# Row norms by a power on GpSimd, and a new order of loads, squares and weight splits, in a two-layer decoder trunk

## The chip, the cores and the metric

The kernel runs on one core of a Trainium2 chip. The metric is the device time of one execution in microseconds (us), as the median of several executions; lower is better. Five engines work side by side, each through its own queue in order: PE (TensorE, matrix products and transposes), ACT (ScalarE), DVE (VectorE), POOL (GpSimd) and SP (SyncE, which here only issues transfers).

## The reference

512 tokens of width 1024 pass two layers. All data are float32.

```python
def rms_norm(x, g):
    y = xf * lax.rsqrt(jnp.mean(xf * xf, axis=-1, keepdims=True) + RMS_EPS)
    return y * g
...
    for layer in range(DEPTH):                  # DEPTH = 2
        if layer == N_CONV_LAYERS:              # layer 1
            k_sh, v_sh = shared_kv(h, positions, kv_norm, w_kv)
        hn = rms_norm(h, mix_norm_pre[layer])
        if layer < N_CONV_LAYERS:
            y = short_conv_mixer(hn, conv_w_in[layer], conv_w[layer], conv_w_out[layer])
        else:
            y = dilated_attention_mixer(hn, positions, k_sh, v_sh, w_q[j], w_o[j])
        h = h + rms_norm(y, mix_norm_post[layer])
        f = swiglu(rms_norm(h, ffn_norm_pre[layer]), ffn_w_gate_up[layer], ffn_w_down[layer])
        h = h + rms_norm(f, ffn_norm_post[layer])
    return h
```

So each token row is normed before and after each mixer and each feed-forward part, and a norm needs one number for each row: one over the root of the mean square. The norm ahead of the shared keys and values is of the same `h` as the one ahead of layer 1, so eight such numbers are needed for each row.

## The kernel before

The 512 tokens stand as four tiles of 128 rows, 0 to 3; the 1024 columns of a tile are worked in two halves, a and b. Every weight is split when it has arrived: `raw` (the load, 1 MB for two matrices' columns), `wh` (a rounded copy that ACT makes, L90) and `wl` (the rest, a subtraction on DVE, L91). Activations are split in the same way into `xh` and `xl`. A product is then three matmuls, `xh` with `wh`, `xh` with `wl` and `xl` with `wh`.

A norm of tile 3, say, goes through four engines. ACT squares the two halves and sums each row (`square`, L190; `ssn` for the sums of a norm behind a block, `ssx` for those of a norm ahead of one). `rsqrt_mean` (L193 to L207) turns the two sums of a row into the reciprocal root: seven small instructions on one number in each of 128 rows, which form the sum `a`, a first guess from the integer bits, and two polishing steps. They run on POOL, but on DVE for tiles 0 and 1 at the start of the program and for tile 3 at its end. DVE then scales the row: `yg` times the result plus `h` (L268) for a norm behind a block, `hn` (L225, or L228 with a gain) for one ahead of a block. PE transposes `hn` (`tr`, L236), and `split` makes `xh` and `xl` of it.

Where one block ends and the next begins (a stage border), the class `Next` runs these steps tile by tile while PE still works on the old block's last tiles. A tile goes through two norms in series there: `add` (the norm of the block's output y, and the residual sum), then `norm` and `x` for the next block. The next block's first products are made in halves: `feature_mms` takes four weight splits ("makers") in turn and makes each one's product for tiles 0 and 1 alone (`between` says where the transposes of tiles 2 and 3 stand, which is behind the second and the fourth of these), then the products for tiles 2 and 3. There are three such borders: convolution to feed-forward (at 197 to 212 us of the profile), feed-forward to attention (563 to 590) and attention to feed-forward (1113 to 1166); the program's start and its end are of the same kind.

Work is put into the queues by a scheduler that goes by its own estimates of times. `behind(marks)` holds a piece of work back, in the order of issue alone, until the instructions in `marks` have been issued. Before, the first pair of makers stood behind tile 0's square and scaling, the second pair behind nothing:

```python
            if i % 2 == 0:
                with behind(marks[i // 2]):
                    pairs += [m() for m in makers[i:i + 2]]
```

At the start, SP issues all loads in the order tile 0 of `h`, the gain row `g0`, `ident` (for the transposes), tile 1, the first weight, and so on. PE runs eight matmuls on zeros (`warm`), spreads `g0` over 128 rows (`g0a`, `g0b`), and runs one more on zeros.

Of the kernel before, what the change touches and what calls it, by code (L numbers as in the profile page):

```python
# [15 lines left out]
P = 128  # L16
T = 512
# [21 lines left out]
def trunk(  # L39
# [42 lines left out]
    cols = keep.tile([P, 64], F32, name="cols")  # L82
    taps, gq, gkv = cols[:, 0:24], cols[:, 24:32], cols[:, 32:40]

    def bank(tag, name):
        return psum.tile([P, T], F32, tag=tag, name=name)

# [52 lines left out]
    @contextmanager  # L140
    def behind(marks):

        with ExitStack() as stack:
            for m in marks:
                stack.enter_context(tc.issue_after(m))
            yield

    def feature_mms(makers, between=None, attn=False, marks=((), ())):

        half = NT // 2
        if between is None:
            pairs = [m() for m in makers]
            for i in range(0, len(pairs), 2):
                feature_mm(pairs[i:i + 2], 0, NT, attn)
            return [ps for ps, _ in pairs]
        pairs = []
        for i in range(len(makers)):
            if i % 2 == 0:  # L160
                with behind(marks[i // 2]):
                    pairs += [m() for m in makers[i:i + 2]]
            feature_mm([pairs[i]], 0, half, attn)
            for f in between[i]:
                f()
# [18 lines left out]

    HALF = [slice(0, 512), slice(512, 1024)]

    def square(pool, y, ssq):
# [5 lines left out]
    def rsqrt_mean(pool, ssq, tag, eng=nc.gpsimd):  # L193
# [12 lines left out]
        eng.tensor_scalar(t, y, a, y, ALU.mult, ALU.mult)  # L206
        eng.tensor_scalar(y, t, -RS ** 10 * 64.0 / 3.0, y, ALU.add, ALU.mult)  # L207
        return y

    def row_gain(pool, g):  # L210
# [2 lines left out]
            nc.sync.dma_start(t, g.partition_broadcast(P))  # L213
        return t

    def norm_x(pool, tt, gain, eng=nc.gpsimd):

        ssq = pool.tile([P, 2], F32, tag="ssx", name="ssx")
        for i, c in enumerate(HALF):
            square(pool, h[:, tt, c], ssq[:, i:i + 1])  # L220
        hn = pool.tile([P, D], F32, tag="hg", name="hn", bufs=3)
        r = rsqrt_mean(pool, ssq, "x", eng)
        for i, c in enumerate(HALF):
            if gain is None:
                nc.vector.tensor_scalar(hn[:, c], h[:, tt, c], r, None, ALU.mult)  # L225
            else:
                g = gain[i] if isinstance(gain, list) else gain[:, c]
                nc.vector.scalar_tensor_tensor(hn[:, c], h[:, tt, c], r, g, ALU.mult, ALU.mult)  # L228
        return hn

    def to_x(tt, hn, attn=False):
# [14 lines left out]
    class Next:  # L246
# [3 lines left out]
        def __init__(self, pool, ys, gpost, gpre, n=0):  # L250
            self.pool, self.ys, self.n = pool, ys, n
            self.gpost, self.gpre = (g if g is None else row_gain(pool, g) for g in (gpost, gpre))
            self.hn, self.ssq, self.yg, self.marks = {}, {}, {}, {}

        def add(self, tt, n, eng=nc.gpsimd):

            y, c = self.ys[tt][n], HALF[n]
            if n == 0:
                self.ssq[tt] = self.pool.tile([P, 2], F32, tag="ssn", name="ssn")
                self.yg[tt] = self.pool.tile([P, D], F32, tag="hg", name="yg", bufs=3)  # L260
            yg = self.yg[tt]
            marks = [square(self.pool, y, self.ssq[tt][:, n:n + 1]),
                     nc.vector.tensor_tensor(yg[:, c], y, self.gpost[:, c], ALU.mult).ins]
            if n == 1:
                self.marks[tt] = marks
                r = rsqrt_mean(self.pool, self.ssq[tt], "n", eng)
                for c in HALF:
                    nc.vector.scalar_tensor_tensor(  # L268
                        h[:, tt, c], yg[:, c], r, h[:, tt, c], ALU.mult, ALU.add)

        def norm(self, tt):
            self.hn[tt] = norm_x(self.pool, tt, self.gpre)

        def x(self, tt):
            to_x(tt, self.hn.pop(tt), self.gpre is None)
# [101 lines left out]
    with ExitStack() as phase:  # L377
# [23 lines left out]
        nc.sync.dma_start(rows[32:40, :], kv_norm.rearrange("(c p) -> c p", p=P))  # L401

        zeros = up.tile([P, T], BF16, name="zeros")
        nc.vector.memset(zeros, 0.0)
        idle = bank("at", "idle")

# [14 lines left out]
        with tc.issue_after(mark):  # L421
            for tt in range(2):
                marks0 = to_x(tt, hn0[tt])
# [6 lines left out]
        for c in range(KT // 2):  # L430
# [346 lines left out]
    with ExitStack() as phase:  # L777
# [23 lines left out]

        class Last(Next):
            def after_half(self, tt, n):
                self.add(tt, n, nc.vector if tt == NT - 1 else nc.gpsimd)
                if n == 1:
                    for c in HALF:
# [48 lines left out]
```

## Time and profile before

| what | value |
|---|---|
| median of 3 executions | 1523.56 us (1521.35 to 1524.08) |
| profiled execution, its own time | 1523.93 us |
| span of the profiled execution, first to last instruction | 1522.1 us |
| PE busy | 1495.3 us, 98% of the span |
| DVE, ACT, POOL busy | 49%, 40%, 7% of the span |
| mean granted TensorE clock | 0.994 |

The span is 1.8 us shorter than the time; that much lies around the first and the last instruction. PE is the engine that is nearly always busy, so what another engine does counts where PE stands still for it, and where PE's clock is lower for having stood still. The granted clock is given as a share of 2.4 GHz; 0.5 is 1.2 GHz.

### The profile page before, as it was taken

The page shows a single profiled execution, that of the slowest core. Times are in us where ns is not written, and L with a number is a line of the kernel's source. Part 1 is how long each engine was busy: PE and PEld are TensorE (multiplying, and loading weights), DVE is VectorE, ACT ScalarE, POOL GpSimd, SP SyncE. Part 2 cuts the span into 40 slices and gives each one's busy share as a digit, 9 for nine tenths or more (in the row PEclk, how much of TensorE's full clock was granted, in tenths as well). Part 3 has the DMA queues.
Part 4 walks back from the last instruction along what each step waited for, and adds up shares of the span by engine and source line. Part 5 has one row for each costly group of instructions (what it writes and reads, how often), then busy time and mean ns, then how long its engine had stood idle before and what let it go on. Part 6 is the DMA issues. An engine that isn't in the chain of part 4 may idle for free.

```text
span 1522.1 us, 20115 instructions
## 1 busy us (share of the span) xinstructions
PE 1495.3 (98%) x8158; PEld 1262.2 (83%) x8158; DVE 745.4 (49%) x1328; ACT 616.4 (40%) x1137; POOL 108.1 (7%) x247
## 2 busy tenths in 40 slices
PE   8999999999999998999999999999998999999997
PEld 7888888888888887898788889889877888888886
DVE  5644453323234366776667566765554322223333
ACT  4323342212123244664666557557553221212321
POOL 2000320000000051000001001000023000000001
PEclk9999999999999999999999999999999999999999
DMA  6333123133323312322112222212040323332311
GB/s 210 111 112 110 56 94 127 62 106 111 124 87 107 111 38 74 111 85 80 61 58 85 84 73 69 84 56 84 30 138 24 124 76 111 111 109 99 111 56 56
DMA packets 109330, 137.43 MB, mean 90 GB/s; under 512 B 3469, under 2 KB 97973, under 8 KB 109238
## 3 DMA queue, kind: packets, MB, share of 16 engines
q1 hardware_dynamic: 107958, 135.89, 27.1%
q8 instruction: 64, 1.05, 0.3%
q0 software_dynamic: 1280, 0.26, 0.2%
q14 instruction: 28, 0.23, 0.0%
HBM read 133.92 MB, written 2.23 MB: 89 GB/s over the span
## 4 chain that ended last, share of the span: by engine, by line
PE 68%; issue 24%; POOL 5%; DVE 1%; ACT 1%; DMA 0%; SPq 0%; DVEq 0%; ACTq 0%; POOLq 0%
PE mmf L137 27%; PE atf L137 14%; PE vps L649 10%; PE s L580 3%; PE o L708 2%; PE tr L679 2%; POOL t L203 1%; POOL a L197 1%; POOL yi L205 1%; POOL q L204 1%; POOL t L206 1%; PE y L182 1%; PE y L180 1%; PE y L178 1%; DVE hn L228 0%
## 5 line engine op out<-in xcount | busy, mean ns | idle before, releaser
L91 DVE TENSOR_TENSOR wl<-raw,wh 128x1024 fp32r<-128x1024 f32 x244 | 292.7, 1222 | 70.7 <-ACT wh L90 70.4
L90 ACT CAST wh<-raw 128x1024 fp32r<-128x1024 f32 x244 | 246.7, 1047 | 100.7 <-PE atf L137 43.1
L137 PE MATMUL mmf<-xh,wh 128*128 128x512 f32 (+1 forms) x848 | 277.4, 380 | 0.2 <-ACT xh L90 0.2
L137 PE MATMUL mmf<-xl,wh 128*128 128x512 f32 (+1 forms) x848 | 271.2, 374 | 0.0
L137 PE MATMUL mmf<-xh,wl 128*128 128x512 f32 (+1 forms) x848 | 271.0, 374 | 0.0
L137 PE MATMUL atf<-xh,wh 128*128 128x512 f32 (+1 forms) x560 | 181.8, 368 | 0.0
L137 PE MATMUL atf<-xl,wh 128*128 128x512 f32 (+1 forms) x560 | 180.1, 365 | 0.0
L137 PEld LDWEIGHTS mmf<-xh,wh 128*128 128x128 f32 x848 | 154.7, 191 | 30.6 <-issue 2.1
L137 PE MATMUL atf<-xh,wl 128*128 128x512 f32 (+1 forms) x560 | 180.0, 365 | 0.0
L362 DVE TENSOR_TENSOR act<-atf,s 128x512 f32<-128x512 f32 x44 | 30.5, 692 | 304.1 <-ACT s L361 304.1
L137 PEld LDWEIGHTS mmf<-xl,wh 128*128 128x128 f32 x848 | 153.2, 188 | 28.8 <-issue 0.9
L137 PEld LDWEIGHTS mmf<-xh,wl 128*128 128x128 f32 x848 | 153.5, 189 | 27.7
L361 ACT ACTIVATE s<-mmf 128x512 f32<-128x512 f32 x44 | 26.3, 598 | 336.3 <-PE mmf L137 336.3
L110 DVE TENSOR_TENSOR raw<-raw,cols 128x512 f32<-128x512 f32 x144 | 90.2, 686 | 78.6 <-DMA raw<-in_w_kv 56.2
L137 PEld LDWEIGHTS atf<-xh,wh 128*128 128x128 f32 x560 | 100.6, 191 | 17.0
L137 PEld LDWEIGHTS atf<-xl,wh 128*128 128x128 f32 x560 | 99.6, 189 | 16.8
L137 PEld LDWEIGHTS atf<-xh,wl 128*128 128x128 f32 x560 | 99.5, 189 | 16.8
L527 ACT COPY sw<-mmf 32x512 f32<-32x512 f32 x92 | 53.3, 579 | 79.4 <-PE mmf L137 72.2
L649 PE MATMUL vps<-wh,xh 128*128 128x256 f32 x384 | 81.1, 289 | 0.0
L649 PE MATMUL vps<-wh,xl 128*128 128x256 f32 x384 | 79.3, 286 | 0.0
L649 PE MATMUL vps<-wl,xh 128*128 128x256 f32 x384 | 79.1, 285 | 0.0
L91 DVE TENSOR_TENSOR al<-act,ah 128x512 fp32r<-128x512 f32 x44 | 30.2, 691 | 93.9 <-ACT ah L90 93.9
(192 smaller groups left out, 2058.6 us busy)
## 6 DMA issues: line engine op xcount, KB each, us to landing
raw<-in_ffn_w_gate_up SPq DMA_DIRECT2D x44, 1024.0 KB, 7.5
raw<-in_w_kv SPq DMA_DIRECT2D x24, 1024.0 KB, 5.2
raw<-in_ffn_w_down SPq DMA_DIRECT2D x22, 1024.0 KB, 4.9
raw<-in_conv_w_in SPq DMA_DIRECT2D x12, 1024.0 KB, 5.2
raw<-in_w_q SPq DMA_DIRECT2D x12, 1024.0 KB, 5.2
raw<-in_conv_w_out SPq DMA_DIRECT2D x4, 1024.0 KB, 4.8
raw<-in_w_o SPq DMA_DIRECT2D x4, 1024.0 KB, 5.0
h<-in_x SPq DMA_DIRECT2D x4, 512.0 KB, 8.9
```

Of the source, the lines that this page charges most:

```text
L90: return [nc.scalar.copy(hi, src).ins, nc.vector.tensor_tensor(lo, src, hi.bitcast(F32), ALU.subtract).ins]
L91: nc.vector.tensor_tensor(lo, src, hi.bitcast(F32), ALU.subtract).ins]
L110: nc.vector.tensor_tensor(src[:, ks], src[:, ks], g.broadcast_to([P, a // 2, b]), ALU.mult)
L137: nc.tensor.matmul(ps, (wh, wl, wh)[p][:, k, :], x[p == 2][:, k], start=i == 0, stop=i == len(todo) - 1)
L178: nc.tensor.matmul(o, ah, wh[i], start=first, stop=False)
L361: nc.scalar.activation(s, ps[2 * j], AF.Silu)
L362: nc.vector.tensor_tensor(act[2 * c + j], ps[2 * j + 1], s, ALU.mult)
L527: nc.scalar.copy(w[s:s + 32], y[s + 32:s + 64])
L580: nc.tensor.matmul(ps[h2][:, b - b2, e * P:(e + 1) * P], q[pr][rw, b * P:(b + 1) * P], k[pr][rw, kb * P:(kb + 1) * P], start=True, stop=True)
L649: nc.tensor.matmul(ps[m][:, n, :], (zh, zh, zl)[p][:, k, 2 * m + n], (wh, wl, wh)[p], start=k == 0 and p == 0, stop=k == KT - 1 and p == 2)
L679: nc.tensor.transpose(tr[:, b - b2, e:e + P], p[:, e - lo:e - lo + P], ident)
L708: m = nc.tensor.matmul(out, v, rhs, start=first, stop=part == 0 and e == 1, skip_group_check=True).ins
```

## The change

It has four parts. (1) `rsqrt_mean` becomes two POOL instructions: the sum `a`, and `a` to the power of -0.5, the exponent being a column of constants (`mhalf`). The rows that DVE took before (tiles 0 and 1 at the start, tile 3 at the end) move to POOL as well. (2) At the start, `g0` and `ident` are issued by ACT; tile 1 of `h` is issued directly behind tile 0; the first weight arrives in two loads of 128 columns each; there are 4 + 2 warming matmuls for 8 + 1; the second half's square of tiles 0 and 1 is made on DVE. (3) Each of the four makers gets a mark of its own: at a border, the first and the second wait as before for tile 0's square and scaling (the first pair did), the third for tile 3's residual sum, the fourth for tile 3's `hn`. (4) The very last output transfer is issued by ACT instead of SP.

```diff
-    def feature_mms(makers, between=None, attn=False, marks=((), ())):
+    def feature_mms(makers, between=None, attn=False, marks=((),) * 4):
...
-                with behind(marks[i // 2]):
-                    pairs += [m() for m in makers[i:i + 2]]
+                for m, mark in zip(makers[i:i + 2], marks[i:i + 2]):
+                    with behind(mark):
+                        pairs.append(m())
...
+        if junk is not None:
+            return nc.vector.tensor_tensor_reduce(
+                junk, y, y, 1.0 / 1024.0, 0.0, ALU.mult, ALU.add, ssq).ins
...
-        eng.tensor_scalar(a, ssq[:, 0:1], EPS, ssq[:, 1:2], ALU.add, ALU.add)
-        yi = pool.tile([P, 1], I32, tag=tag + "y", name="yi")
-        eng.tensor_scalar(yi, a.bitcast(I32), -0.5, -553033664.0, ALU.mult, ALU.add)
-        y = yi.bitcast(F32)
-        t = pool.tile([P, 1], F32, tag=tag + "t", name="t")
-        q = pool.tile([P, 1], F32, tag=tag + "q", name="q")
-        eng.tensor_scalar(t, y, a, y, ALU.mult, ALU.mult)
-        eng.tensor_scalar(q, t, -RS ** 2 * 10.0 / 3.0, t, ALU.add, ALU.mult)
-        eng.tensor_scalar(y, q, RS ** 4 * 5.0, y, ALU.add, ALU.mult)
-        eng.tensor_scalar(t, y, a, y, ALU.mult, ALU.mult)
-        eng.tensor_scalar(y, t, -RS ** 10 * 64.0 / 3.0, y, ALU.add, ALU.mult)
+        nc.gpsimd.tensor_scalar(a, ssq[:, 0:1], EPS, ssq[:, 1:2], ALU.add, ALU.add)
+        y = pool.tile([P, 1], F32, tag=tag + "y", name="y")
+        nc.gpsimd.tensor_tensor(y, a, mhalf, ALU.pow)
         return y
...
-                    "marks": [self.marks[0], ()]}
+                    "marks": [self.marks[0]] * 2 + [[self.added[NT - 1]], self.normed[NT - 1]]}
...
+        nc.scalar.dma_start(g0, mix_norm_pre[0:1, :])
+        nc.scalar.dma_start(ident, consts[:, 0:P])
         for tt in range(NT):
             nc.sync.dma_start(h[:, tt, :], x[0, tt * P:(tt + 1) * P, :])
-            if tt == 0:
-                nc.sync.dma_start(g0, mix_norm_pre[0:1, :])
-                nc.sync.dma_start(ident, consts[:, 0:P])
             if tt == 1:
-                first.append(load_cols(w, D))
+                raw = wp.tile([P, KT, 256], F32, tag="raw", name="raw")
+                for j in range(2):
+                    cs = slice(j * P, (j + 1) * P)
+                    latest[:] = [nc.sync.dma_start(
+                        raw[:, :, cs], w[:, D:][:, cs].rearrange("(k p) n -> p k n", p=P)).ins]
+                first.append(raw)
...
-        with tc.issue_after(warm(8)):
+        with tc.issue_after(warm(4)):
...
-            mark = warm(1)
-
-        hn0 = [norm_x(npool, tt, gain0, nc.vector) for tt in range(2)]
+            mark = warm(2)
+
+        hn0 = [norm_x(npool, tt, gain0, (None, junk)) for tt in range(2)]
...
-                marks=[(), marks0])
+                marks=[()] + [marks0] * 3)
...
-                self.add(tt, n, nc.vector if tt == NT - 1 else nc.gpsimd)
+                self.add(tt, n)
...
-                        nc.sync.dma_start(out[0, tt * P:(tt + 1) * P, c], h[:, tt, c])
+                    for q, c in zip((nc.sync, nc.scalar if tt == NT - 1 else nc.sync), HALF):
+                        q.dma_start(out[0, tt * P:(tt + 1) * P, c], h[:, tt, c])
```

The order of instructions moves in more places than the diff names, since the scheduler decides anew. Three of them follow; line numbers are those of each kernel's own source, so that L190 of before is L199 of after (the square), and L90 is L93 (the casts).

ACT at the start of the program, before (`ssx` are the row sums of `h`):

```order
L190 ACT_TABLE_LOAD
L190 ACTIVATE junk,ssx<-h 128x512 x4
L90 CAST wh<-raw 128x1024 x2
L90 CAST xh<-tr 128x512 x4
L190 ACTIVATE junk,ssx<-h 128x512 x3
```

and after:

```order
L396 DMA g_104<-in_mix_norm_pre 1x1024
L397 DMA ident<-in_consts 128x128
L199 ACT_TABLE_LOAD
L199 ACTIVATE junk,ssx<-h 128x512 x2
L93 CAST wh<-raw 128x1024
L93 CAST xh<-tr 128x512 x4
L93 CAST wh<-raw 128x1024
L199 ACTIVATE junk,ssx<-h 128x512 x3
```

Two loads now stand ahead of the table load, two of the four squares are gone from ACT, and only one weight cast stands ahead of the four casts of the transposed rows.

ACT at the border from feed-forward to attention, before (`y3a` and `y3b` are the halves of tile 3 of the feed-forward output):

```order
L190 ACTIVATE junk,ssn<-y3a 128x512
L90 CAST xh<-tr 128x16x32 x2
L90 CAST wh<-raw 128x1024 x3
L190 ACTIVATE junk,ssn<-y3b 128x512
L90 CAST wh<-raw 128x1024
L90 CAST xh<-tr 128x16x32 x2
L190 ACTIVATE junk,ssx<-h 128x512 x2
L90 CAST xh<-tr 128x16x32 x2
```

and after:

```order
L199 ACTIVATE junk,ssn<-y3a 128x512
L93 CAST xh<-tr 128x16x32 x2
L199 ACTIVATE junk,ssn<-y3b 128x512
L199 ACTIVATE junk,ssx<-h 128x512 x2
L93 CAST wh<-raw 128x1024
L93 CAST xh<-tr 128x16x32 x3
L93 CAST wh<-raw 128x1024 x3
L93 CAST xh<-tr 128x16x32
```

The three weight casts ahead of the square of `y3b` have moved behind both norms of tile 3. On DVE the same place has, before, four `wl` ahead of the residual sum of tile 3 and eight scalings of raw weights (L110) ahead of its `hn`; after, the residual sum stands directly behind `yg` of `y3b`, two of the eight scalings stand ahead of `hn`, and the `wl` behind it.

PE at the same border, before, from tile 2's transposes on (`mmf` are the first two products, `atf` the third and the fourth):

```order
L236 MATMUL tr<-ident,hn 128x128 x8
L137 MATMUL atf<-xh,wh 128x4x64 x8
L137 MATMUL atf<-xh,wl 128x4x64 x8
L137 MATMUL atf<-xl,wh 128x4x64 x8
L137 MATMUL atf<-xh,wh 128x4x64 x8
L137 MATMUL atf<-xh,wl 128x4x64 x8
L137 MATMUL atf<-xl,wh 128x4x64 x8
L236 MATMUL tr<-ident,hn 128x128 x8
```

and after:

```order
L239 MATMUL tr<-ident,hn 128x128 x12
L140 MATMUL atf<-xh,wh 128x4x64 x8
L140 MATMUL mmf<-xh,wh 128x4x64 x8
L140 MATMUL atf<-xh,wl 128x4x64 x8
L140 MATMUL atf<-xl,wh 128x4x64 x8
L140 MATMUL atf<-xh,wh 128x4x64 x10
L239 MATMUL tr<-ident,hn 128x128 x4
```

Half of tile 3's eight transposes now stand directly behind tile 2's, ahead of the third and the fourth product, and the other half inside the fourth.

ACT at the border from attention to feed-forward, before (each `ssn<-y_...` is one half of a tile of the attention's output, in the order tile 0 to tile 3, so two of them are a tile):

```order
L190 ACTIVATE junk,ssn<-y_9424 128x512
L90 CAST wh<-raw 128x1024
L190 ACTIVATE junk,ssx<-h 128x512
L90 CAST xh<-tr 128x512 x2
L90 CAST wh<-raw 128x1024
L190 ACTIVATE junk,ssx<-h 128x512
L190 ACTIVATE junk,ssn<-y_9107 128x512
L190 ACTIVATE junk,ssn<-y_9425 128x512
L90 CAST xh<-tr 128x512 x2
```

and after, from the same square of tile 1 on:

```order
L199 ACTIVATE junk,ssn<-y_9283 128x512
L199 ACTIVATE junk,ssx<-h 128x512 x2
L199 ACTIVATE junk,ssn<-y_8966 128x512
L199 ACTIVATE junk,ssn<-y_9284 128x512
L93 CAST xh<-tr 128x512 x2
L199 ACTIVATE junk,ssx<-h 128x512 x2
L199 ACTIVATE junk,ssn<-y_8967 128x512
L93 CAST xh<-tr 128x512
L199 ACTIVATE junk,ssn<-y_9285 128x512
L93 CAST xh<-tr 128x512 x2
```

No weight cast stands between the squares of tile 1 any more, and the second pair of `xh` casts (tile 1's) now stands behind the squares of tile 3 (`y_8967` and `y_9285`).

## Rows read from the trace of the kernel before

**Rows 1.** The page: busy us, share and instructions of each engine.
```profile
PE 1495.3 (98%) x8158; PEld 1262.2 (83%) x8158; DVE 745.4 (49%) x1328; ACT 616.4 (40%) x1137; POOL 108.1 (7%) x247
```
**Rows 2.** What PE waited for: total us, times, longest us.
```profile
PE tr L236 <- DVE hn L228: 10.3, 8, 3.9
PE tr L236 <- DVE hn L225: 5.8, 1, 5.8
```
**Rows 3.** Stretches: length, busy PE, PEld, DVE, ACT, POOL, clock, DMA share, GB/s.
```profile
212.00:520.00 308.00, 308.00 (x1405) 256.97 (x1406) 101.66 (x105) 83.81 (x104) 0.00 (x0) 1.00 0.32 105
583.00:590.00 7.00, 7.00 (x44) 6.76 (x43) 1.38 (x2) 0.70 (x2) 0.00 (x0) 0.73 0.01 2
1142.60:1166.00 23.40, 17.59 (x128) 16.31 (x128) 12.65 (x20) 8.00 (x21) 10.81 (x35) 0.93 0.00 1
```
**Rows 4.** The timeline of the start: start us, us, instruction, idle time before it.
```profile
0.74 0.38 SPq L393 DMA_DIRECT2D h<-in_x  x1
...
1.95 0.43 SPq L393 DMA_DIRECT2D h<-in_x  x1
...
7.59 0.63 ACT L190 ACTIVATE junk<-h 128x512 bf16<-128x512 f32 x1 [2.20 <-DMA h<-in_x]
...
14.61 2.08 PE L137 MATMUL mmf<-xh,wh 128*128 128x256 f32 x8
...
26.60 1.38 PE L236 MATMUL tr<-ident,hn 128*128 128x128 f32 x8 [1.24 <-DVE hn L228]
```
**Rows 5.** The timeline of POOL: one reciprocal root alone, one instruction beside DVE.
```profile
178.26 0.29 POOL L197 TENSOR_SCALAR a<-ssx 128x1 f32<-128x1 f32 x1 [2.36 <-ACT junk L190]
...
178.94 0.35 POOL L203 TENSOR_SCALAR t<-yi,a 128x1 f32<-128x1 f32 x1
...
180.56 0.27 POOL L207 TENSOR_SCALAR yi<-t,yi 128x1 f32<-128x1 f32 x1
...
199.81 2.32 POOL L203 TENSOR_SCALAR t<-yi,a 128x1 f32<-128x1 f32 x1
```
**Rows 6.** The timeline of the border from convolution to feed-forward.
```profile
210.52 1.32 PE L236 MATMUL tr<-ident,hn 128*128 128x128 f32 x8 [1.24 <-DVE hn L228]
```
**Rows 7.** The timeline of the border from feed-forward to attention.
```profile
562.37 0.39 PE L182 MATMUL y3b<-wh,al 128*128 128x512 f32 x1
...
566.11 0.61 ACT L190 ACTIVATE junk<-y3b 128x512 bf16<-128x512 f32 x1
...
566.90 1.45 POOL L197 TENSOR_SCALAR a<-ssn 128x1 f32<-128x1 f32 x1 [2.41 <-ACT junk L190]
...
572.50 1.41 DVE L268 SCALAR_TENSOR_TENSOR h<-yg,yi,h 128x512 f32<-128x512 f32 x2 [1.35 <-POOL yi L207]
...
580.52 0.27 POOL L207 TENSOR_SCALAR yi<-t,yi 128x1 f32<-128x1 f32 x1
...
581.37 1.97 PE L236 MATMUL tr<-ident,hn 128*128 128x128 f32 x8 [5.77 <-DVE hn L225]
```
**Rows 8.** The timeline of the border from attention to feed-forward.
```profile
1135.96 1.33 PE L236 MATMUL tr<-ident,hn 128*128 128x128 f32 x8 [0.39 <-DVE hn L228]
...
1142.40 0.39 PE L182 MATMUL y<-wh,xl 128*128 128x512 f32 x1
...
1146.69 1.97 PE L236 MATMUL tr<-ident,hn 128*128 128x128 f32 x8 [3.91 <-DVE hn L228]
...
1163.83 1.32 PE L236 MATMUL tr<-ident,hn 128*128 128x128 f32 x8 [1.39 <-DVE hn L228]
```
**Rows 9.** The timeline of the end, on DVE.
```profile
1515.67 0.20 DVE L197 TENSOR_SCALAR a<-ssn 128x1 f32<-128x1 f32 x1
...
1517.47 1.41 DVE L268 SCALAR_TENSOR_TENSOR h<-yg,yi,h 128x512 f32<-128x512 f32 x2
```
**Rows 10.** The page's groups: the two instructions of a weight split.
```profile
L91 DVE TENSOR_TENSOR wl<-raw,wh 128x1024 fp32r<-128x1024 f32 x244 | 292.7, 1222 | 70.7 <-ACT wh L90 70.4
L90 ACT CAST wh<-raw 128x1024 fp32r<-128x1024 f32 x244 | 246.7, 1047 | 100.7 <-PE atf L137 43.1
```

More of the change, by code (lines that the diff above doesn't have):

```diff
@@ L83, in trunk @@
     taps, gq, gkv = cols[:, 0:24], cols[:, 24:32], cols[:, 32:40]
+    mhalf = keep.tile([P, 1], F32, name="mhalf")
+    nc.vector.memset(mhalf, -0.5)
     def bank(tag, name):
@@ L185, in trunk, with square @@
     HALF = [slice(0, 512), slice(512, 1024)]
-    def square(pool, y, ssq):
+    def square(pool, y, ssq, junk=None):
+        if junk is not None:
+            return nc.vector.tensor_tensor_reduce(
+                junk, y, y, 1.0 / 1024.0, 0.0, ALU.mult, ALU.add, ssq).ins
         junk = pool.tile([P, 512], BF16, tag="junk", name="junk")
@@ L191, in square, with rsqrt_mean @@
             junk, y, AF.Square, scale=1.0 / 32.0, accum_out=ssq).ins
-    def rsqrt_mean(pool, ssq, tag, eng=nc.gpsimd):
+    def rsqrt_mean(pool, ssq, tag):
         a = pool.tile([P, 1], F32, tag=tag + "a", name="a")
-        eng.tensor_scalar(a, ssq[:, 0:1], EPS, ssq[:, 1:2], ALU.add, ALU.add)
-        yi = pool.tile([P, 1], I32, tag=tag + "y", name="yi")
-        eng.tensor_scalar(yi, a.bitcast(I32), -0.5, -553033664.0, ALU.mult, ALU.add)
-        y = yi.bitcast(F32)
-        t = pool.tile([P, 1], F32, tag=tag + "t", name="t")
-        q = pool.tile([P, 1], F32, tag=tag + "q", name="q")
-        eng.tensor_scalar(t, y, a, y, ALU.mult, ALU.mult)
-        eng.tensor_scalar(q, t, -RS ** 2 * 10.0 / 3.0, t, ALU.add, ALU.mult)
-        eng.tensor_scalar(y, q, RS ** 4 * 5.0, y, ALU.add, ALU.mult)
-        eng.tensor_scalar(t, y, a, y, ALU.mult, ALU.mult)
-        eng.tensor_scalar(y, t, -RS ** 10 * 64.0 / 3.0, y, ALU.add, ALU.mult)
+        nc.gpsimd.tensor_scalar(a, ssq[:, 0:1], EPS, ssq[:, 1:2], ALU.add, ALU.add)
+        y = pool.tile([P, 1], F32, tag=tag + "y", name="y")
+        nc.gpsimd.tensor_tensor(y, a, mhalf, ALU.pow)
         return y
@@ L214, in row_gain, with norm_x @@
         return t
-    def norm_x(pool, tt, gain, eng=nc.gpsimd):
+    def norm_x(pool, tt, gain, junk=(None, None), marks=None):
         ssq = pool.tile([P, 2], F32, tag="ssx", name="ssx")
         for i, c in enumerate(HALF):
-            square(pool, h[:, tt, c], ssq[:, i:i + 1])
+            square(pool, h[:, tt, c], ssq[:, i:i + 1], junk[i])
         hn = pool.tile([P, D], F32, tag="hg", name="hn", bufs=3)
-        r = rsqrt_mean(pool, ssq, "x", eng)
+        r = rsqrt_mean(pool, ssq, "x")
         for i, c in enumerate(HALF):
             if gain is None:
-                nc.vector.tensor_scalar(hn[:, c], h[:, tt, c], r, None, ALU.mult)
+                mark = nc.vector.tensor_scalar(hn[:, c], h[:, tt, c], r, None, ALU.mult)
             else:
                 g = gain[i] if isinstance(gain, list) else gain[:, c]
-                nc.vector.scalar_tensor_tensor(hn[:, c], h[:, tt, c], r, g, ALU.mult, ALU.mult)
+                mark = nc.vector.scalar_tensor_tensor(
+                    hn[:, c], h[:, tt, c], r, g, ALU.mult, ALU.mult)
+        if marks is not None:
+            marks[:] = [mark.ins]
         return hn
@@ L252, in __init__, with add @@
             self.gpost, self.gpre = (g if g is None else row_gain(pool, g) for g in (gpost, gpre))
-            self.hn, self.ssq, self.yg, self.marks = {}, {}, {}, {}
-        def add(self, tt, n, eng=nc.gpsimd):
+            self.hn, self.ssq, self.yg = {}, {}, {}
+            self.marks, self.added, self.normed = {}, {}, {}
+        def add(self, tt, n):
             y, c = self.ys[tt][n], HALF[n]
@@ L265, in add @@
                 self.marks[tt] = marks
-                r = rsqrt_mean(self.pool, self.ssq[tt], "n", eng)
+                r = rsqrt_mean(self.pool, self.ssq[tt], "n")
                 for c in HALF:
-                    nc.vector.scalar_tensor_tensor(
-                        h[:, tt, c], yg[:, c], r, h[:, tt, c], ALU.mult, ALU.add)
+                    self.added[tt] = nc.vector.scalar_tensor_tensor(
+                        h[:, tt, c], yg[:, c], r, h[:, tt, c], ALU.mult, ALU.add).ins
         def norm(self, tt):
-            self.hn[tt] = norm_x(self.pool, tt, self.gpre)
+            self.hn[tt] = norm_x(self.pool, tt, self.gpre, marks=self.normed.setdefault(tt, []))
         def x(self, tt):
@@ L403, in trunk @@
         zeros = up.tile([P, T], BF16, name="zeros")
+        junk = up.tile([P, T], BF16, name="junk")
         nc.vector.memset(zeros, 0.0)
@@ L803, in after_half @@
             def after_half(self, tt, n):
-                self.add(tt, n, nc.vector if tt == NT - 1 else nc.gpsimd)
+                self.add(tt, n)
                 if n == 1:
-                    for c in HALF:
-                        nc.sync.dma_start(out[0, tt * P:(tt + 1) * P, c], h[:, tt, c])
+                    for q, c in zip((nc.sync, nc.scalar if tt == NT - 1 else nc.sync), HALF):
+                        q.dma_start(out[0, tt * P:(tt + 1) * P, c], h[:, tt, c])
         ffn(1, pending, lambda ys: Last(npool, ys, ffn_norm_post[1], None))
```

## The prediction

> **What bounds the kernel now.** I read the page first. PE is busy for 1495.3 of 1522.1 us [rows 1], so at most 26.8 us of standing still can be won, and beside them what PE loses by running at its lower clock. The change takes next to nothing from PE's own work (three warming matmuls that nothing waits for), so all else depends on where those 26.8 us lie. The list of what PE waited for puts 16.1 of them on one thing, transposes (`tr`) waiting for a normed row (`hn`) from DVE: 10.3 us in eight waits, and one of 5.8 us [rows 2]. A table by stretch then shows that they are at the stage borders alone: from 212 to 520 us PE is busy for every one of 308.00 us at clock 1.00, while 583 to 590 runs at 0.73 on the mean, and 1142.6 to 1166 is busy for 17.59 of 23.40 us at 0.93 [rows 3]. The rest of the standing still is the start, before PE's first work, and the last 8 us, behind its last. So each border is a race: PE uses up the products that it can make without tile 3 (or tile 1), while tile 3 goes in series through square, reciprocal root, residual sum, square, reciprocal root and `hn`. I therefore walked each border twice, once with before's times and once with the order and the lengths of the changed kernel.
>
> **The reciprocal root.** Alone on POOL the seven instructions take from 178.26 to 180.56 + 0.27, that is 2.57 us [rows 5]; the last of a row of instructions before the next starts some 0.09 us on. The first, `a` (0.29 us), stays. No row here shows a power. From below it can't well be shorter than one instruction with two multiplications on the same 128 numbers, 0.35 us; from above I take the whole sequence that it replaces, 2.57 - 0.38 = 2.2 us [rows 5]. A power is a logarithm, a product and an exponential, and nothing between them leaves the instruction, so I value it near the lower end, as three instructions of about 0.27 us: 0.8 us. A root then takes 0.29 + 0.09 + 0.8 = 1.18 us, 1.4 us less than before. Beside DVE's two-input work the sequence stretches: one instruction of 0.35 us took 2.32 us at 199.81 [rows 5], and in the border to attention the first norm of tile 3 needs from 566.90 until `h` starts at 572.50, 5.6 us [rows 7], where 2.57 would do. Two instructions can be hit twice where seven can be hit seven times. The Trainium skill (SBUF — State Buffer, SBUF: two separate sides) says that GpSimd and a DVE instruction with two SBUF inputs exclude each other for a whole instruction; the row agrees, and by that rule the new root could at worst be held up by one weight split at each of its two instructions.
>
> **The start: 3.0 us.** SP issues tile 1 of `h` at 1.95 us, 1.21 behind tile 0; without the two issues between, it goes out 0.38 us behind [rows 4], and two small transfers are out of its way. Its landing (the square starts at 7.59) I put at 6.3, between 5.4 and 7.59. One half's square is left on ACT, and the other runs beside it on DVE, so the root is there at about 8.4. DVE then has three halves of `hn` to make, ending at about 10.5; the second half's transposes and the casts that follow put the first product at 12.55 (12.0 to 13.0) in place of 14.61 [rows 4]: 2.06 us. The weight's first 128 columns land and are split before that. With the roots of tiles 2 and 3 shorter, the wait of 1.24 us at 26.60 [rows 4] goes as well; 0.3 us are kept back for a transpose that now waits for its cast. Bounds: -1 to 4.5 us. The four warming matmuls that are gone cover nothing but the wait for `g0`; if that lands no earlier, PE idles in their place at no cost.
>
> **Convolution to feed-forward: 1.2 us.** The one wait, 1.24 us at 210.52 [rows 6], ends with the root of tile 3; two roots of 1.4 us less each remove it with 1.6 us to spare. The fourth weight split, now behind `hn`, must be ready at 206.2 and is at 204.6.
>
> **Feed-forward to attention: 8.3 us.** The last matmul of tile 3 ends at 562.76, but ACT squares its second half only at 566.11, behind three weight casts of 1.05 us each [rows 7, 10]; these stand behind it in the new order. So: square at 562.8, root 563.7 to 564.9, residual sum 564.95 to 566.4, squares until 567.2 (the first starts when half of `h` is there), root 567.3 to 568.5, then `hn` and the transposes at about 569.4, in place of 580.52 for the root's last instruction and 581.37 for the transpose [rows 7]. Before, these transposes stood behind the third and the fourth product, which PE had done at 575.60 (581.37 - 5.77); in the new order half of them stand directly behind tile 2's, and two products of 3 us each earlier PE is there at about 569.6. So `hn` is in time by little; if it is late by some tenths, PE waits those, as its queue is in order. The wait of 5.77 us goes. With it goes the clock's fall: 583 to 590 at 0.73 [rows 3] is 7.00 x 0.27 = 1.9 us lost, and 581.37 to 583 at half speed another 0.8. Together 5.77 + 2.7 - 0.2 = 8.3. What is late next is the third and the fourth weight split, put behind tile 3 now: two casts and two `wl` in turn, 1.05 and 1.22 us each [rows 10], give the third `wl` at 572.2, which is when it is needed, and the fourth at 575.4 against 576.5. The margin is 0 to 1.1 us.
>
> **Attention to feed-forward: 5.3 us.** PE stands still for 0.39, 3.91 and 1.39 us for three transposes [rows 8], 5.7 us, and the clock of 0.93 over 23.40 us costs 1.65 [rows 3]: 7.3. The chain of tile 0 and that of tile 1 are in series through POOL, two roots each, and all four get shorter, so those waits go. A new one takes part of their place. The last matmul of the attention output starts at 1142.40 [rows 8] and ends 0.39 later; in the new order the casts of tile 1's rows to `xh` stand on ACT behind the squares of tile 3, which need that matmul, and the first product needs these casts: some 0.4 for the release, 0.8 for a square, 0.6 for a cast and 0.2, 2.0 us. Thus 7.3 - 2.0 = 5.3. If the clock falls after this wait as it does after the 3.91, 1.7 us less.
>
> **The end: 1.1 us.** The root on DVE takes from 1515.67 to 1517.47, 1.80 us [rows 9]. On POOL it is 1.18, and it starts beside the last scaling on DVE, behind which it stood, not after it: 1.1. The last transfer on a second queue: 0 to 0.1, counted as nothing.
>
> **Sum.** 3.0 + 1.2 + 8.3 + 5.3 + 1.1 = 18.9 us off the profiled execution's 1523.9: 1505.0. That execution is 0.4 us above the median of the three shown, which doesn't matter here.
>
> **The rivals.** A change below 0.2% (3 us) can't be told from none in this kernel.
>
> *The power costs about as much as the sequence (2.2 us).* For: it is one of the bounds, and an instruction of POOL that computes no simple arithmetic may be a loop. Against: nothing. Each root is then 1.4 us longer than forecast. The two roots of tile 3 put `hn` at the border to attention 2.8 us later, of which 2.3 are not covered, and the clock's 2.7 come back: 5.0; 3.0 at the next border, 1.4 at the start and 1.2 at the end. 10.6 us less: 1515.6.
>
> *The weight splits take over as the wait.* For: the margin of 0 to 1.1 us above, with two splits in place of four ready ahead. Against: ACT and DVE have no other work there. A wait of 2 us in the border to attention, with the clock's fall of 2.7: 1509.7.
>
> *The first power comes late.* In before POOL makes its first root at 16 us and nothing shows whether anything had to be fetched first; in the changed kernel PE waits for one from about 5 us on. If the first root were delayed by up to the 11 us between, the first product would come at 14.6 to 21.7: 1507 to 1514, taken as 1510. The Trainium skill (GPSIMD Engine Reference, 2.1 Instruction dispatch) says that the first call of newly loaded code on GpSimd costs about 6 us which no row shows; by that, my estimate would be 1509. No run here shows it.
>
> *Slower than before.* One mechanism: a still longer power. Every microsecond more costs 10.6 / 1.4 = 7.6 us, because two roots in series stand on the path at each border. So 18.9 us are used up at 0.8 + 2.5 = 3.3 us; with 4 us the time is 1529. For: no row shows a power. Against: POOL's instructions with nothing in their way take 0.35 us at most in the chain [rows 5], a tenth of that.
>
> **How the numbers follow.** Forecast 55%, power as long as the sequence 12%, weight splits 15%, late first power 9%: these are faster, 0.91. Slower 0.05; a power near 3.3 us, with no change that can be told, 0.04. The forecast's own range is 1500 to 1509, from the bounds of the start (5.5 us between them), the possible fall of the clock at the second border and a power of 0.35 us. The range 1497 to 1516 reaches up to the power of 2.2 us and down to where all of PE's 26.8 us between matmuls would be gone.
>
> **What would show it.** The power's own row: 0.8 us, and its largest value beside DVE. The first product at 12.0 to 13.0 us. No wait above 0.5 us for `hn` at the border to attention, and a clock of 1.00 there; if the clock stays low, the rivals on the splits or the long power are right, and the releaser (`wl` or `hn`) tells which. At the border to feed-forward one wait of about 2 us, released by `xh`. The last residual sum starts 1.1 us earlier behind the last square than before. I would be wrong above all if the power isn't near 0.8 us.

## The result, and the profile after

The changed kernel takes 1498.55 us (median of 4, 1497.63 to 1499.31), the kernel before 1522.64 us in the same comparison: a ratio of 0.984, 95% interval 0.982 to 0.986. That is 24.1 us less and 6.5 us below the forecast of 1505.0. It lies inside the range of 1497 to 1516, near its lower end, and 1.5 us below the range of 1500 to 1509 that the prediction gave for its forecast alone. The spans of the two profiled executions are 1522.1 and 1497.0 us, 25.1 us apart.

The page of the changed kernel answers to [rows 1]:

```profile
span 1497.0 us, 19969 instructions
PE 1484.5 (99%) x8155; PEld 1256.2 (84%) x8155; DVE 741.6 (50%) x1312; ACT 615.6 (41%) x1133; POOL 58.2 (4%) x108
```

PE made three matmuls less, and yet it was busy for 10.8 us less: for the most part because matmuls that had run at the lower clock now ran at the upper. POOL's work is halved. The list of what PE waited for, against [rows 2]:

```profile
PE mmf L140 <- ACT xh L93: 2.8, 3, 1.4
PE idle L418 <- DVE u L452: 1.3, 1, 1.3
PE y L183 <- ACT xh L93: 0.7, 1, 0.7
PE y L185 <- DVE wl L94: 0.5, 1, 0.5
PE tr L239 <- DVE hn L228: 0.4, 1, 0.4
```

Of 16.1 us of waiting for `hn`, 0.4 are left. A new line stands on top: three waits of 2.8 us in all for the casts of the transposed rows. The root itself, as POOL's groups (line, names, count, busy, mean ns) and its timeline at the border to attention show it:

```profile
L207 POOL TENSOR_TENSOR y<-a,mhalf 128x1 f32<-128x1 f32 x32 | 18.8, 588 | 2.7
```
```profile
557.54 0.30 POOL L205 TENSOR_SCALAR a<-ssn 128x1 f32<-128x1 f32 x1 [4.81 <-ACT junk L199]
...
557.92 0.56 POOL L207 TENSOR_TENSOR y<-a,mhalf 128x1 f32<-128x1 f32 x1
558.52 1.41 DVE L272 SCALAR_TENSOR_TENSOR h<-yg,y,h 128x512 f32<-128x512 f32 x2 [0.35 <-POOL y L207]
```

A power takes 0.56 us, here at most 0.84 beside DVE's work; a root takes 0.94 (557.54 to 558.48) in place of 2.57 [rows 5], 1.63 us less. DVE takes up its result 0.04 us later.

To see where the 25.1 us came from, I cut both traces at the start of the last matmul of each block: the convolution's (196.52 before, 190.69 after), the first feed-forward's (562.37 [rows 7], 556.26), the attention's (1142.40 [rows 8], 1125.74), the second feed-forward's (1513.86, 1490.10). Of each border, the first norms fall into the stretch ahead of the cut, the rest into the one behind. The same cuts are made in the experiments:

| us | start to convolution | to feed-forward 1 | to attention | to feed-forward 2 | to the end | span |
|---|---|---|---|---|---|---|
| before | 196.52 | 365.85 | 580.03 | 371.46 | 8.24 | 1522.1 |
| after | 190.69 | 365.57 | 569.48 | 364.36 | 6.90 | 1497.0 |
| e1, old root | 195.97 | 365.12 | 571.78 | 370.55 | 8.88 | 1512.3 |
| e2, power alone | 194.88 | 364.40 | 570.11 | 364.99 | 6.92 | 1501.3 |
| e3, no late marks | 190.78 | 364.39 | 568.80 | 365.08 | 6.95 | 1496.0 |
| e4, old start | 195.12 | 365.37 | 569.67 | 364.29 | 6.95 | 1501.4 |
| e5, two powers | 192.35 | 363.90 | 569.56 | 367.69 | 7.90 | 1501.4 |

So the change gave 5.8 us at the start, 0.3 in the stretch with the first border, 10.6 in that with the second, 7.1 in that with the third and 1.3 at the end. The stretches over the second and the third border, with the columns of [rows 3]:

```profile
555.00:575.00 20.00, 20.00 (x162) 19.60 (x161) 12.77 (x19) 8.11 (x14) 1.88 (x4) 1.00 0.30 96
1105.00:1135.00 30.00, 28.86 (x164) 25.01 (x163) 20.73 (x31) 16.70 (x40) 8.24 (x15) 1.00 0.18 58
```

PE no longer stands still at the second border, and the clock stays at its upper level in both.

### The profile page after: what moved, and what is told of

It is laid out like the page before. It is cut to its first block, busy times and chain, and to the rows that moved or that the text cites. A ratio compares the mean times of both kernels' runs of the same rounds, so it can differ in the third digit from the quotient of the medians.

```text
span 1497.0 us, 19969 instructions
## 1 busy us (share of the span) xinstructions
PE 1484.5 (99%) x8155; PEld 1256.2 (84%) x8155; DVE 741.6 (50%) x1312; ACT 615.6 (41%) x1133; POOL 58.2 (4%) x108
## 4 chain that ended last, share of the span: by engine, by line
PE 66%; issue 26%; DMA 3%; DVE 2%; POOL 1%; ACT 1%; POOLq 0%; DVEq 0%; SPq 0%; ACTq 0%
PE mmf L140 26%; PE atf L140 14%; PE vps L658 8%; PE s L589 2%; PE o L717 2%; PE tr L688 2%; DMA raw<-in_w_kv 1%; DVE raw L113 1%; DMA raw<-in_ffn_w_gate_up 1%; POOL y L207 1%; DMA raw<-in_w_q 1%; DVE wl L94 1%; POOL a L205 1%; PE y1b L187 0%; PE y1a L183 0%
## 5 line engine op out<-in xcount | busy, mean ns | idle before, releaser
L93 ACT CAST wh<-raw 128x1024 fp32r<-128x1024 f32 x244 | 246.8, 1047 | 104.3 <-PE atf L140 42.7
```

Of the source, the lines that this page charges most:

```text
L93: return [nc.scalar.copy(hi, src).ins, nc.vector.tensor_tensor(lo, src, hi.bitcast(F32), ALU.subtract).ins]
```

## The experiments

Two theories stood against each other. "Root": the borders wait because the reciprocal root, twice in series for each tile, is long. "Order": they wait because weight casts stand ahead of tile 3's squares on ACT. The start was a question apart.

**e1: the changed kernel with the old root.**

```diff
-        nc.gpsimd.tensor_tensor(y, a, mhalf, ALU.pow)
+        yi = pool.tile([P, 1], I32, tag=tag + "y", name="yi")
+        nc.gpsimd.tensor_scalar(yi, a.bitcast(I32), -0.5, -553033664.0, ALU.mult, ALU.add)
...
+        nc.gpsimd.tensor_scalar(y, t, -RS ** 10 * 64.0 / 3.0, y, ALU.add, ALU.mult)
```

> The changed kernel with the seven-instruction reciprocal root put back, on POOL for every tile; start, marks and end stay as changed. If the length of the root is what decides at the borders (theory 'root'), each root is again 1.6 us longer alone and up to 4 us longer beside DVE's splits: 3 to 6 us with the clock's fall at the border from feed-forward to attention, 3 to 5 at the next, 2 at the start, 1.6 at the end: 1508 to 1513. If the order of squares and weight splits decides (theory 'order'), tile 3's work still runs ahead of the splits and only start and end lose: 1501 to 1504.

1515.79 us, ratio to before 0.996 (0.994 to 0.997): 17.2 us of the 24 are gone, more than either theory said. What PE waited for:

```profile
PE tr L247 <- DVE hn L236: 6.5, 6, 1.7
PE mmf L140 <- DVE wl L94: 1.9, 1, 1.9
PE atf L140 <- ACT wh L93: 1.4, 1, 1.4
```

The table says where, for the profiled execution, which was the fastest of the four and is 15.3 us longer than that of the changed kernel: 5.3 us at the start, 2.3 in the stretch with the second border, 6.2 in that with the third, 2.0 at the end. At the second border the old root loses little as long as tile 3's squares stand ahead of the casts. There PE no longer waits for `hn`, but 1.41 us for a weight cast (`wh`) and 0.68 us for `xh`; the six waits for `hn` lie at the start and at the third border, where the new order does not help.

**e2: the kernel before with the power alone.** The seven lines of `rsqrt_mean` are replaced by the two of the change, for all tiles on POOL; nothing else.

> The kernel before with the power alone (two POOL instructions for every root); loads, squares, marks and end as before, so that three weight casts stand ahead of tile 3's second square again. Theory 'root': from the square of y3b at 566.1 on, two roots of 0.95 us put hn at about 571, ahead of the 575.6 at which PE wants it, so the wait of 5.8 us goes without any new order, and most waits of the attention border too: 1504 to 1509. Theory 'order': half of the gain at most, 1511 to 1516.

1502.76 us, ratio 0.987 (0.986 to 0.989). The power alone gives 19.4 of the 24.1 us, and all of the gain behind the start: from the convolution's end on, e2's stretches sum to 1306.42 us and those of the changed kernel to 1306.31. At the second border, in the order of before, with the square of `y3b` still behind three casts:

```profile
560.51 0.58 ACT L193 ACTIVATE junk<-y3b 128x512 bf16<-128x512 f32 x1
...
561.29 1.12 POOL L200 TENSOR_SCALAR a<-ssn 128x1 f32<-128x1 f32 x1 [5.55 <-ACT junk L193]
...
568.43 0.85 POOL L202 TENSOR_TENSOR y<-a,mhalf 128x1 f32<-128x1 f32 x1
569.98 0.87 DVE L220 TENSOR_SCALAR hn<-h,y 128x512 f32<-128x512 f32 x2
...
571.88 1.03 PE L231 MATMUL tr<-ident,hn 128*128 128x128 f32 x8
```

POOL's instructions are stretched beside DVE's work (1.12 and 0.85 us in these rows), and `hn` is still made from 569.98 on, ahead of PE's transposes at 571.88, which don't wait for it. Theory "root" holds.

**e3: the changed kernel without the late marks.**

```diff
-                    "marks": [self.marks[0]] * 2 + [[self.added[NT - 1]], self.normed[NT - 1]]}
+                    "marks": [self.marks[0]] * 2 + [(), ()]}
```

> The changed kernel without the marks that hold the third and the fourth weight split behind tile 3's residual sum and hn (the first two keep theirs); the order on ACT at the border from feed-forward to attention is again that of before. Theory 'root': the short root needs no such order, 1498 to 1500. Theory 'order': waits for hn come back at two borders, with the clock's fall: 1503 to 1508.

1497.94 us (1497.76 to 1498.08), ratio 0.984 (0.983 to 0.986): the same as the changed kernel. So part (3) of the change is worth nothing beside the power; by the table it costs 1.2 and 0.7 us in the stretches with the first and the second border and gives 0.7 in that with the third. Theory "order" fell.

**e4: the changed kernel with the start of before.** Loads, warming matmuls, squares and marks of the start as before; the roots are powers.

> The changed kernel with the start of before (g0 and ident issued by SP between tiles 0 and 1, one load for the first weight, 8 + 1 warming matmuls, all squares on ACT, splits not held), but roots by the power. If loads and squares make the start's gain of 5.8 us, the first product is back at about 13.5 us and the time at 1502 to 1504. If the short root makes it, 1499 to 1500.

1503.36 us, ratio 0.988 (0.986 to 0.989): 4.8 us lost, 4.4 of them at the start. Now the start has four corners: neither part 196.52, new loads and squares alone (e1) 195.97, power alone (e4) 195.12, both 190.69. Alone they give 0.6 and 1.4 us, together 5.8. PE's timeline of the changed kernel,

```profile
1.34 1.89 PE L418 MATMUL idle<-zeros 128*128 128x512 bf16 x4 [1.34 <-DVE u L452]
...
5.03 1.91 PE L425 MATMUL g0b<-g,ones 1*128 1x512 f32 x2
...
7.69 2.99 PE L239 MATMUL tr<-ident,hn 128*128 128x128 f32 x16
10.44 0.72 PE L140 MATMUL mmf<-xh,wh 128*128 128x256 f32 x4
...
11.98 1.12 PE L140 MATMUL mmf<-xh,wl 128*128 128x256 f32 x8
```

and that of e4 show why:

```profile
5.88 1.02 PE L421 MATMUL g0b<-g,ones 1*128 1x512 f32 x2
...
7.46 0.66 PE L239 MATMUL tr<-ident,hn 128*128 128x128 f32 x4 [0.24 <-DVE hn L228]
10.36 2.82 PE L239 MATMUL tr<-ident,hn 128*128 128x128 f32 x12 [2.25 <-DVE hn L228]
13.59 3.16 PE L140 MATMUL mmf<-xh,wh 128*128 128x256 f32 x12 [0.40 <-ACT xh L93]
```

In the changed kernel PE works from 1.34 us to 11.16 us without a stop and then waits only 0.25 us; its early work (`g0b`) is at the lower rate, but its first products follow each other at some 0.12 us (2.4 GHz). In e4 the same two matmuls of `g0b` took 1.02 us in place of 1.91, so there the upper level came earlier. But PE then stood still for 2.25 us from 8.1 on, the granted clock went from 1.00 to 0.50 between 8.25 and 8.50 us and stayed there until 18.5, and 12 transposes took 2.82 us and the next 12 matmuls 3.16, some 0.24 us each (1.2 GHz). In the first microseconds, until the clock first changes, the profile's clock column is no guide: it says 1.00 in the changed kernel too, where `g0b` ran at the lower rate. There the level is read from the matmuls.

**e5: two powers in a row** (0.5, then -1).

> The changed kernel with two powers in a row (0.5, then -1: the same value), so that a root takes 0.56 + 0.09 = 0.65 us more on POOL, 1.6 us in all. Theory 'the root is on the path at every border': 7 to 10 us for each us of root, so 1503 to 1505. Theory 'the power has slack left': at the border to attention PE has no wait in the changed kernel, so only the end (0.65), the start (about 0.7) and the border to feed-forward (0.7) get longer: 1500 to 1501.

1503.25 us, ratio 0.988 (0.986 to 0.989): 4.7 us for 0.65 us of root, 7.2 us for each. It is not spread over all borders. The start lost 1.7 us, which the next stretch won back; that with the second border stayed as it was (0.1), so the power has slack there; 3.3 us went at the third border and 1.0 at the end. At the third, one wait got longer,

```profile
1130.05 1.02 PE L142 MATMUL mmf<-xh,wh 128*128 128x256 f32 x4 [2.96 <-ACT xh L95]
```

in place of 1.15 us, and the clock fell behind it (stretch with the columns of [rows 3]):

```profile
1126.20:1136.20 10.00, 7.04 (x48) 6.80 (x45) 8.10 (x13) 4.89 (x14) 3.75 (x7) 0.83 0.00 0
```

**e6: the changed kernel with 8 + 1 warming matmuls** (`warm(8)` and `warm(1)` for `warm(4)` and `warm(2)`).

> The changed kernel with 8 + 1 warming matmuls in place of 4 + 2. Theory 'clock': in the runs with eight, the clock stood at its upper level from 5.9 us on, and here no wait follows in which it could fall, so the g0 products and the transposes run at full speed and the first product comes no later: 1497.5 to 1498.5. Theory 'the fewer warming matmuls are what lets g0 be ready earlier': hn waits for the second half of g0, first product 0.5 to 1 us later: 1499 to 1500.

1502.54 us, ratio 0.987 (0.986 to 0.988): worse than both theories had it. The scheduler had also put a `wl` between the halves of `hn`:

```profile
8.74 1.23 DVE L94 TENSOR_TENSOR wl<-raw,wh 128x1024 fp32r<-128x1024 f32 x1 [0.30 <-ACT wh L93]
...
9.88 1.40 DVE L228 SCALAR_TENSOR_TENSOR hn<-h,y,g0b 128x512 f32<-128x512 f32 x2
...
10.68 1.97 PE L239 MATMUL tr<-ident,hn 128*128 128x128 f32 x8 [1.31 <-DVE hn L228]
```

The clock had risen by 6 us (`g0b` took 1.02 us) and fell again before this wait: PE stood still for 0.59 us up to 8.49, and the granted clock is 1.00 up to 8.75 and 0.50 from 9.0 to 15.5 us, so that the 8 transposes behind the wait of 1.31 us took 1.97. The convolution ended 2.3 us later. The run says nothing on the number of warming matmuls by itself.

**e7 and e8: the waits ahead of the transposes filled with warming matmuls**, in e4 (12 for 1) and in the kernel before (6 for 1).

> The run with the old start and the power, with 12 warming matmuls behind g0 in place of 1, which fill the time from 7 to 9.5 us in which PE stood still for 2.2 us and after which the next 24 matmuls ran at half speed. Theory 'clock': no fall, first products at 0.12 us a matmul, 1.5 to 3 us won: 1500.5 to 1502. Theory 'loads': the row's arrival sets it, 1503 to 1504.

> The kernel before with 6 warming matmuls behind g0 in place of 1, nothing else. Theory 'clock': PE doesn't stand still for 1.22 us at 9.2, the first products come at 0.12 in place of 0.21 us a matmul, 1 to 2 us won: 1520.5 to 1521.5. Rival: the transposes are put off by the extra work and nothing is won: 1522 to 1523.

e7: 1502.61 us (ratio 0.987, 0.986 to 0.989), not to be told from e4's 1503.36. e8: 1523.61 (ratio 1.001, 1.000 to 1.002), no gain. In e7 the transposes and the first products ran at the upper level, as the theory said, but at the price of what it saved:

```profile
8.58 4.96 PE L414 MATMUL idle<-zeros 128*128 128x512 bf16 x12
13.37 1.91 PE L239 MATMUL tr<-ident,hn 128*128 128x128 f32 x16
15.13 1.73 PE L140 MATMUL mmf<-xh,wh 128*128 128x256 f32 x12
```

These 12 warming matmuls ran at the lower level (0.41 us each), held the transposes until 13.37 where e4 began the last 12 at 10.36, and only then came the upper level. In e8 PE stood still for 2.59 us all the same. In neither run did the filling pay: in e7 it ended later than the wait that it filled, in e8 earlier.

**e10 and e11: the start's parts**, in the changed kernel: `g0` and `ident` issued by SP behind tile 0 again; all squares on ACT again.

> The changed kernel with g0 and ident issued by SP between tiles 0 and 1 again; all else as changed. If the earlier landing of tile 1 is what the start needs, its square starts at about 7.5 in place of 5.8, PE stands still before the second tile's transposes for over 1 us, the next matmuls run at half speed, and the time is 1501 to 1503. If the loads count for their issue time alone, 0.7 us: 1499 to 1499.5.

> The changed kernel with all squares on ACT again (tiles 0 and 1); all else as changed. Each of the two roots is ready some 0.7 us later, so that PE stands still for some 0.7 us ahead of the transposes. If it is a wait of that size which brings the clock's lower level with it, 1500 to 1501.5; if not, 1499.

e10: 1500.90 us (ratio 0.986, 0.985 to 0.988); the convolution ends at 192.09, 1.4 us later, with the first product at 12.42 in place of 10.44 and a wait of 0.82 us for `g0`. Its profiled execution, with a span of 1497.3, was the fastest of its four, so of the 2.4 us between the medians the trace explains 1.4. e11: 1499.33 (ratio 0.985, 0.984 to 0.987), the convolution's end at 191.12, 0.4 us later; its longest stop of PE in the start was 0.24 us, not 0.7, so it didn't test a wait of that size.

**e9 and e12: tile 1's transposes half a tile earlier at the third border**, without the late marks (e9) and with them (e12).

```diff
-        pending = Next(npool, ys, mix_norm_post[1], ffn_norm_pre[1], 1)
+        pending = Next(npool, ys, mix_norm_post[1], ffn_norm_pre[1], 0)
```

> The run without the late marks, and with tile 1's transposes at the border from attention to feed-forward allowed behind the first half of tile 3's output instead of the second (n = 0 in place of 1). There PE still waits 1.35 us, for casts of tile 1 that stand behind tile 3's squares on ACT; with the short root tile 1's hn is there at 1122 us, four us before PE needs it. If that order is the cause, the wait goes: 1496.3 to 1497.0. If the transposes now hold PE up inside the old block, nothing is won: 1497.9 to 1499.

> The changed kernel, late marks kept, with the same early transposes. The wait of 1.15 us at 1128 goes: 1497.0 to 1497.6; the wait of 1.4 us at 205.8 (tile 3's casts behind a weight cast that waits for its load) stays, and sets it apart from the run without the marks.

e9: 1501.34 us (ratio 0.987, 0.985 to 0.988), e12: 1503.70 (0.988, 0.987 to 0.990), both slower than the changed kernel. The number moves tile 0's transposes too, which I had overlooked, and in e9 PE now waited for them inside the old block:

```profile
1114.89 1.32 PE L239 MATMUL tr<-ident,hn 128*128 128x128 f32 x8 [3.21 <-DVE hn L228]
```

The clock fell behind it (0.51 from 1116.25 to 1119.5 us). The wait of 1.35 us at the end of the border did go in e9, and that of 1.15 us in e12; but in e12 PE waited 2.37 us for `hn` in the old block, again with a fall of the clock, and at the first border 2.48 us in place of 1.41, which the edit doesn't touch. No run beat the changed kernel by more than the measurement can tell.

## Why the prediction came out as it did

The sum came out 6.2 us short of the 25.1 us between the two profiled executions, mostly because two of its five terms, the start and the border from attention to feed-forward, were too small by 2.8 and 3.9 us, while that of the first border was 0.9 us too large. These errors do not cancel. That the time still lies in the range of 1497 to 1516 is owed to the range's width, and 1.7 us of the surplus can't be credited to the change (below).

**The root.** The mechanism held: e2 shows that the shorter root alone makes 19.4 us. The power was put at 0.8 us and took 0.56. "Every microsecond more costs 7.6 us" was 7.2 in e5 and 17.2 / 1.63 = 10.6 in e1; that it came about through "two roots in series at each border" was too even, since e5 cost nothing at the second border. The root of 0.94 us is 0.24 shorter than the 1.18 of the prediction, and at these prices that is some 1.7 to 2.5 us of the difference.

**The start, 3.0 forecast, 5.8 measured.** This term was mis-sized. The first product came at 10.44, not at 12.0 to 13.0. Tile 1 landed earlier still (its square started at 5.83, not 6.3), its root was there at 7.77, not 8.4, and, what I hadn't counted, PE no longer stopped, so that the transposes' second half and the first products ran at the upper clock. e1, e4 and the changed kernel show that both parts are needed for this.

**Convolution to feed-forward, 1.2 forecast, 0.3 measured.** The wait for `hn` went as said. What I missed is the wait that took its place, on ACT's queue in the changed kernel:

```profile
204.16 1.04 ACT L93 CAST wh<-raw 128x1024 fp32r<-128x1024 f32 x1 [1.96 <-DMA raw<-in_ffn_w_gate_up]
205.12 1.07 ACT L93 CAST xh<-tr 128x512 fp32r<-128x512 f32 x2
```
```profile
205.75 0.39 PE L140 MATMUL mmf<-xh,wh 128*128 128x256 f32 x1 [1.41 <-ACT xh L93]
```

A weight cast, waiting for its load, stands ahead of tile 3's casts, and PE waits 1.41 us where it had waited 1.24 [rows 6]. In e3, where the casts come first, PE waits 0.24 at this place and the stretch is 1.2 us shorter. The prediction had checked the wrong thing here: it asked when the fourth weight split is ready, took 204.6 for it, and didn't ask what stands behind it on ACT. The split's cast began only at 204.16, when the load was there, and its `wl` ended at 206.47.

**Feed-forward to attention, 8.3 forecast.** All of the 5.77 us and the clock's fall [rows 7, 3] are gone, 8.4 us by the rows. The size was right, and the reason half so: I let the moved squares and the short root share it, but e2 shows that the power alone does it, and e1 that the new order with the old root does most of it too (a stretch of 571.78 against 580.03 us). The rival on the weight splits did not come in the changed kernel: the margin that I gave as 0 to 1.1 us held. In e1, behind the old root, such a wait did come (1.41 us for `wh`).

**Attention to feed-forward, 5.3 forecast.** The cuts give 10.55 - 8.4 = 2.1 us ahead of the attention's last matmul and 7.1 behind it, 9.2 in all. This term was mis-sized in three places, and the reason given for one of them was wrong. The new wait was there, released by `xh` as forecast, but 1.15 us long, not 2.0:

```profile
1125.66 0.63 ACT L199 ACTIVATE junk<-h 128x512 bf16<-128x512 f32 x1 [3.53 <-DVE h L272]
...
1126.96 0.58 ACT L199 ACTIVATE junk<-y 128x512 bf16<-128x512 f32 x1
...
1127.53 0.57 ACT L93 CAST xh<-tr 128x512 fp32r<-128x512 f32 x1
```
```profile
1128.15 0.74 PE L140 MATMUL mmf<-xh,wh 128*128 128x256 f32 x4 [1.15 <-ACT xh L93]
```

The prediction derived it from the attention's last matmul, which tile 3's squares need. But only the second half's square needs it, and that one stands behind the first cast. Ahead of the cast ACT stood still for 3.53 us until tile 2's residual sum `h` was there, then made two squares of `h` and one of tile 3's first half. In e3 no square of tile 3 stands ahead of the casts, and PE waits all the same:

```profile
1126.59 0.74 PE L140 MATMUL mmf<-xh,wh 128*128 128x256 f32 x4 [1.35 <-ACT xh L93]
```

There ACT waited 2.58 us for the same `h`, made its square at 1125.34 and the casts from 1125.97 on. So it is tile 2's chain that the product waits for, with a root in it. This also fits e5, where the longer root put this square at 1127.56, after 4.17 us of standing still, and the wait at 2.96.

A fourth wait for `hn`, of 0.49 us, went too; with 3.91, 1.39, 1.65 and less the 1.15 that makes 6.3 of the 7.1 us, and 0.8 stay unassigned. And some 1.7 us can't be credited to the change: just ahead of this border, where both kernels wait 0.7 and 0.5 us for other things, the clock fell in the profiled execution of before and not in that of the changed kernel. These are stretches of 9.7 us that end 19.8 us ahead of the end of the attention's last matmul, before and after:

```profile
1113.29:1122.99 9.70, 9.14 (x30) 6.65 (x31) 5.93 (x6) 4.67 (x7) 0.00 (x0) 0.82 0.75 244
```
```profile
1096.63:1106.33 9.70, 8.52 (x55) 6.40 (x55) 5.92 (x6) 5.55 (x8) 0.00 (x0) 1.00 0.57 201
```

In e6, e7 and e11 it fell there as well, with the same two waits, and in the other nine runs it didn't. What decides it stays open. With the 0.39 us of [rows 8] the 1.7 make up the 2.1 us ahead of the attention's last matmul.

**The end, 1.1 forecast, 1.3 measured.** The root runs beside the last scaling and is 0.24 us shorter than I took it; the last residual sum starts 1.76 us behind the start of the last square, where it had been 3.13.

**The rivals.** The power as long as the sequence, and the still longer one, fell with the first power's row of 0.56 us. The late first power did not come either: the first root is made at 5.17 to 6.13 us, the power in it 0.57 us long. The Trainium skill (GPSIMD Engine Reference, 2.1 Instruction dispatch) gives about 6 us for the first call of newly loaded code; whether this power is such a call no run shows, and the trace has no such delay at it. The 1509 that the prediction gives for this case has no working; 6 us on top of 1505.0 would be 1511.

## What to carry to other kernels

Look for a short serial chain that many tiles pass at every stage border, and shorten it before rearranging what stands around it: here the short root made the new order at the borders worthless. Where PE's clock falls after a wait, a microsecond won from the chain can be worth more than one, and two edits that each leave a gap can give little alone and much together. After such a change look at what the engine waits for next at the same place: here a cast that stood behind a weight that hadn't arrived, and one that stood behind another tile's squares.

## What the runs showed of the hardware that I had not expected

The power on GpSimd is no slower than two of the simple instructions it replaces (0.56 us against 0.27 to 0.35). GpSimd's instructions were held up by DVE's two-input work in every kernel (0.30 to 1.45 us for the same `a` in the changed kernel, up to 2.32 in e5). The power was held up seldom: 0.84 us at most in the changed kernel, up to 0.86 in the others, and once 1.57 for the second power of e5. The clock does not behave the same way in each execution of the same work: behind the same 8 warming matmuls it stood at its upper level by 6 us in e2, e4, e6 and e8 (`g0b`'s two matmuls took 1.02 us), and not before 13 us in e7 and in the profiled execution of before (1.91 us). Nor did the length of a wait alone decide whether it fell: 1.92 us in e1 and 2.48 in e12 passed without a fall, and after 0.7 and 0.5 us it fell in four of fourteen traces.
